# A hybrid decoder layer on one core: sums of y for the output projection from one load of each pair, and DRAM copies in rows of 8 KB

## The chip, the core and the metric

The kernel runs on one core of a Trainium2 chip. The core has five engines, each with its own queue of instructions that it works off in order: TensorE (PE; its weight loads are PEld) multiplies matrices into PSUM, VectorE (DVE) and ScalarE (ACT) do elementwise work, GpSimd (POOL) does some too and starts the DMAs that add into memory, and SyncE (SP) starts most of the other DMAs. Sixteen DMA engines move the data between DRAM and the on-chip memory (SBUF). The metric is the device time of one execution in microseconds, lower is better.

## The reference

One layer on 512 tokens with a model width of 2048, float32 throughout. Cut to what matters here:

```
h     = rms_norm(x, norm_w) * (1 + scale) + shift      # scale, shift, gate from c @ w_ada
proj  = h @ w_in                                       # split into aq ak av ag d_qkv dz db da mg_a mg_b
a_out = swa_attention(...) * silu(ag)
y_a   = a_out @ w_o_swa
o     = gated_delta_rule(...)                          # 32 value heads, chunks of 64 tokens
y_b   = (rms_norm(o) * silu(dz)) @ w_o_dn
y     = sigmoid(mg_a) * y_a + sigmoid(mg_b) * y_b      # 512 x 2048
out   = x + gate * (y @ w_out)                         # the output projection
```

## The kernel before

Each float32 factor of a large matmul is split in two, a high part (a rounding copy on ScalarE, line 52) and the rest (a subtraction on VectorE, line 53), and a product is three matmuls (`mm3`, lines 240 to 242): high by high, high by low, low by high. Weights come in tiles of 128 x 2048 (1 MB, `raw`, two buffers, line 200), are split in halves of 1024 columns (`whi`, `wlo`, three buffers), and every half feeds eight steps of 128 rows.

The stages in order: startup (adaLN, norm, first projections); DeltaNet (`deltanet`); the product with w_o_dn (`branch_b`); window attention (`attention`); `finish`. In the second part of DeltaNet the heads run in sixteen groups. While the matmuls of group g+1 stream, a chain of small scan steps of group g (`scan`: pp, pv, pd, po) is laid between them. `pump`, called after every six matmuls, advances such generators, and a generator with a rate advances only on a part of the calls.

One of these is `weight_sums`, started at group 2 with a rate of 0.13. It first copies x to the output in four DRAM-to-DRAM copies of 1 MB (line 671). Then it builds the summed weight quadrants of the output projection in DRAM (`ws_d`): for each of four parts two copies of a quadrant (line 684), two accumulating DMAs from GpSimd (line 688), one copy and one accumulation, and again one of each: 16 copies of 1 MB. They stand in SyncE's queue among the weight loads.

The output projection multiplies y (quadrants a11, a12 for the first 256 tokens, a21, a22 for the others, by halves of the 2048 columns) with w_out in seven products in place of eight, over two halves of the output columns n: m1 to m7 in the order of `out_order`, with a11, a12, the sums s3, s1, s2, then a22 and the sum s4. Each product is four items of twelve matmuls of 512 columns.

`finish` has two parts. The first, sixteen times, makes a tile of y: it loads the gate and the other branch's tile, takes the product with w_o_swa (`channel_tile`), combines them on VectorE (lines 1332, 1333), writes the tile to DRAM (`y_d`, line 1334), and splits its first 256 columns into a11 or a12; for the first eight tiles it also makes s3. s1, s2, s4 and a22 go to the memory of h (`hh`, `hl`), which is free only as the last of these products ends. So they are made in the second part, `output`, by `combos`, a generator that advances once per item: two passes over eight pairs of y tiles. GpSimd loads a pair from DRAM (line 1359, `ya` and `yc`, two buffers each), the first pass makes s1 and s2, the second loads the pair again and makes s4, and splits a22. An item's weights are split two items ahead by `prep`, and `out_load` (line 1395) loads w_out or its sums into three buffers. `evict` and `columns` combine the products, multiply with the gate and add into the output by DMA.

The order of the instructions on each engine isn't that of the code. A planner sets it when the program is built: it takes instructions in order of priority as they become ready by its own idea of how long things take, and allots the buffers. The blocks under `behind` (the scan steps, `weight_sums`) may not go ahead of the last matmul traced. On the chip each engine then keeps the order that was set, whatever is ready.

Of the kernel before, what the change touches and what calls it, by code (L numbers as in the profile page):

```python
# [36 lines left out]
class Layer:  # L37
# [628 lines left out]
    def weight_sums(self):  # L666

        nc = self.nc
        for t in range(NTB):
            s = slice(t * P, (t + 1) * P)  # L670
            nc.sync.dma_start(out=self.out[s], in_=self.a["x"][s])
            yield
        for n in range(2):
            for i in range(2):
                w = lambda c, r: self.a["w_out"][2 * c + n, 2 * r + i]
                m7, m5, m6, m4 = (self.ws_d[s, n, i] for s in ("m7", "m5", "m6", "m4"))
                steps = [
                    [(m7, w(1, 0), w(1, 1)), (m5, w(0, 0), w(1, 0))],
                    [(m6, m7, w(0, 0))],
                    [(m4, m6, w(0, 1))],  # L680
                ]
                for parts in steps:
                    for dst, src, _ in parts:
                        nc.sync.dma_start(out=dst, in_=src)
                    for _ in range(2):
                        yield
                    for dst, _, more in parts:
                        nc.gpsimd.dma_start(out=dst, in_=more, accum_op=ALU.add, max_dma_last_dim=8192)
                    for _ in range(2):
                        yield  # L690
# [621 lines left out]
    def finish(self):  # L1312
        tc, nc, a = self.tc, self.nc, self.a
        with ExitStack() as es:
            yp = es.enter_context(tc.tile_pool(name="fy", bufs=1, reuse_waits="tile"))
            wk = es.enter_context(tc.tile_pool(name="fwk", bufs=2, reuse_waits="tile"))
            quad = lambda pool, name: tuple(pool.tile([P, 8, 256], F32R, name=name + x) for x in "hl")
            A = {n: quad(yp, n) for n in ("a11", "s3", "a12")}
            self.wtiles, self.wnext = {}, 0
            self.wpool = es.enter_context(tc.tile_pool(name="fraw", bufs=3, reuse_waits="tile"))  # L1320
            for _ in range(3):
                self.out_load()
            lo, hi = slice(0, 256), slice(256, 512)
            with ExitStack() as eo:
                self.pmm = eo.enter_context(tc.tile_pool(name="pmmf", bufs=2, space=PSUM, reuse_waits="tile"))
                for j in range(KT):
                    m = wk.tile([P, T], F32, tag="m", name="m")
                    nc.sync.dma_start(out=m, in_=self.ma_d[j])
                    yb = wk.tile([P, T], F32, tag="yb", name="yb")
                    nc.sync.dma_start(out=yb, in_=self.yb_d[j])  # L1330
                    ps = self.channel_tile(f"os{j}")
                    nc.vector.scalar_tensor_tensor(out=m, in0=m, scalar=1.0, in1=ps, op0=ALU.add, op1=ALU.mult)
                    nc.vector.tensor_tensor(out=m, in0=m, in1=yb, op=ALU.add)
                    nc.sync.dma_start(out=self.y_d[j], in_=m)
                    h, l = A["a11" if j < 8 else "a12"]
                    self.split(h[:, j % 8, :], l[:, j % 8, :], m[:, lo])
                    if j < 8:
                        h, l = A["s3"]
                        nc.vector.tensor_tensor(out=yb[:, lo], in0=m[:, lo], in1=m[:, hi], op=ALU.add)
                        self.split(h[:, j, :], l[:, j, :], yb[:, lo])  # L1340
            v = lambda i: (self.hh[:, 4 * i : 4 * i + 4, :], self.hl[:, 4 * i : 4 * i + 4, :])
            for i, n in enumerate(("s1", "s2", "s4", "a22")):
                A[n] = tuple(x.rearrange("p a (b t) -> p (a b) t", b=2) for x in v(i))
            self.output(es, wk, A)

    def combos(self, wk, A):

        nc = self.nc
        lo, hi = slice(0, 256), slice(256, 512)
        TT = nc.vector.tensor_tensor  # L1350
        steps = [(second, kt) for second in range(2) for kt in range(8)]
        pairs = {}

        def load(i):
            if i < len(steps):
                kt = steps[i][1]
                for j, tag in enumerate(("ya", "yc")):
                    t = wk.tile([P, T], F32, tag=tag, name=tag)
                    nc.gpsimd.dma_start(out=t, in_=self.y_d[kt + 8 * j])
                    pairs[i, j] = t  # L1360

        load(0)
        load(1)
        yield
        for i, (second, kt) in enumerate(steps):
            p, q = pairs.pop((i, 0)), pairs.pop((i, 1))
            TT(out=p[:, hi], in0=p[:, hi], in1=q[:, hi], op=ALU.subtract)
            if second:
                TT(out=p[:, lo], in0=p[:, hi], in1=p[:, lo], op=ALU.add)
                TT(out=p[:, lo], in0=p[:, lo], in1=q[:, lo], op=ALU.subtract)  # L1370
                self.split(A["a22"][0][:, kt, :], A["a22"][1][:, kt, :], q[:, hi])
            else:
                nc.vector.scalar_tensor_tensor(
                    out=p[:, lo], in0=p[:, hi], scalar=-1.0, in1=p[:, lo], op0=ALU.mult, op1=ALU.subtract
                )
                self.split(A["s1"][0][:, kt, :], A["s1"][1][:, kt, :], p[:, hi])
            n = "s4" if second else "s2"
            self.split(A[n][0][:, kt, :], A[n][1][:, kt, :], p[:, lo])
            load(i + 2)
            yield  # L1380

    def out_order(self):
        return [
# [4 lines left out]
    def out_load(self):  # L1388
        j = self.wnext
        if j < 28:  # L1390
            n, m, i = j // 14, j // 2 % 7, j % 2
            name, _, q = self.out_order()[m]
            t = self.wpool.tile([P, 2048], F32, tag="raw", name="raww")
            src = self.a["w_out"][2 * q[0] + n, 2 * q[1] + i] if q else self.ws_d[name, n, i]
            self.nc.sync.dma_start(out=t, in_=src)
            self.wtiles[j] = t
            self.wnext += 1

    def output(self, es, wk, A):
# [7 lines left out]
        def prep(i):  # L1407
# [6 lines left out]
            if i % 2:  # L1414
                del self.wtiles[i // 2]
                self.out_load()

        side = self.combos(wk, A)
        next(side, None)
        todo = []  # L1420
# [15 lines left out]
        def evict(n, name):  # L1436
            TT = nc.vector.tensor_tensor
            for t in range(2):
                b = ps[name, t]
                if (n, name) == (1, "m4"):  # L1440
                    last[t] = wk.tile([P, T], F32, tag="yb", name="x")
                    nc.sync.dma_start(out=last[t], in_=a["x"][t * P : (t + 1) * P, 1024 + T : 2048])
                if name == "m1":
                    o = t * 1024 + n * T
                    nc.sync.dma_start(out=gt[:, t, :], in_=self.gate_d[o : o + T].partition_broadcast(P))
                if name in ("m1", "m5"):
                    k = wk.tile([P, T], F32, tag=f"{name}{t}", name=name, bufs=1)
                    nc.scalar.copy(out=k, in_=b)
                    keep[name, t] = k
                elif name == "m2":  # L1450
                    c = wk.tile([P, T], F32, tag="m", name="c11")
                    TT(out=c, in0=b, in1=keep["m1", t], op=ALU.add)
                    columns(n, 0, t, c, 1.0)
                elif name == "m6":
                    u1, u5 = keep["m1", t], keep["m5", t]
                    u = wk.tile([P, T], F32, tag="m", name="u2")
                    TT(out=u, in0=b, in1=u1, op=ALU.add)
                    TT(out=u1, in0=ps["m7", t], in1=u, op=ALU.add)
                    c = wk.tile([P, T], F32, tag="m", name="c22")
                    TT(out=c, in0=u1, in1=u5, op=ALU.add)  # L1460
                    TT(out=u5, in0=u, in1=u5, op=ALU.add)
                    columns(n, 1, 2 + t, c, 1.0)
                elif name == "m4":
                    k = keep["m1", t]
                    TT(out=k, in0=b, in1=k, op=ALU.subtract)
                    columns(n, 0, 2 + t, k, 1.0)
                elif name == "m3":
                    k = keep["m5", t]
                    TT(out=k, in0=b, in1=k, op=ALU.add)
                    columns(n, 1, t, k, -1.0, last.get(t) if n else None)  # L1470
# [133 lines left out]
```

## Time and profile before

| | us |
|---|---|
| median of 3 runs | 2958.47 (2956.22 to 2960.14) |
| the profiled execution | 2958.95 |
| its span, first to last instruction | 2956.1 |
| TensorE busy | 2884.4 |
| VectorE busy | 1750.1 |
| ScalarE busy | 1084.5 |
| GpSimd busy | 250.7 |

The mean granted clock of TensorE is 0.99 of full speed. A row of a timeline gives the start in us from the span's start, the duration, the engine, the line of the kernel, the operation with the tile it writes and those it reads, the shape, how many such instructions were merged, and in brackets how long the engine had been idle and what ended the idle time. A row of a group gives the number of instructions, then busy us and mean ns of one, then the idle time before them; or, in the view of a tile, the shortest, median and longest duration in ns. SPq stands for SyncE's queue of DMAs. A row of a stretch gives the busy time and, in parentheses, the number of instructions of each engine.

### The profile page before, as it was taken

What the parts mean: (1) busy time and instruction counts of PE and PEld (TensorE: products, weight loads), DVE (VectorE), ACT (ScalarE), POOL (GpSimd) and SP (SyncE); (2) the same over time, 40 slices, a digit from 0 to 9 for tenths busy, and PEclk for the clock granted to TensorE, in tenths of its full rate; (3) what the DMA queues carried; (4) which work ended last, traced back from release to release, by engine and by line L of the source; (5) the groups of instructions that cost most, each with busy time, mean ns of one, the idle gap of its engine ahead of it and who ended that gap; (6) DMA issues with size and microseconds to landing.
All of it is one profiled execution on the core that took longest, in us unless ns stands there. A gap on an engine that the chain in (4) does not pass through costs nothing.

```text
span 2956.1 us, 38061 instructions
## 1 busy us (share of the span) xinstructions
PE 2884.4 (98%) x14556; PEld 2359.3 (80%) x14556; DVE 1750.1 (59%) x2885; ACT 1084.5 (37%) x2113; POOL 250.7 (8%) x250
## 2 busy tenths in 40 slices
PE   8899999999899999999999999999999999999999
PEld 6677888887688888888888788888788788888777
DVE  7775998776677554545544453433755655554575
ACT  4354334332234433333333322311334434432343
POOL 0022211100101111110000000000100000000110
PEclk9999999999899999999999999999999999999999
DMA  9747555635456655754332575545322223365585
GB/s 384 278 147 222 168 155 168 190 110 183 146 156 181 201 181 158 205 157 140 113 123 87 200 265 195 200 165 165 105 83 99 76 88 111 109 249 181 175 250 170
DMA packets 175656, 497.78 MB, mean 168 GB/s; under 512 B 72978, under 2 KB 75538, under 8 KB 135602
## 3 DMA queue, kind: packets, MB, share of 16 engines
q1 hardware_dynamic: 168594, 466.52, 46.8%
q0 software_dynamic: 6880, 28.84, 4.7%
q8 instruction: 114, 1.87, 0.3%
q14 instruction: 68, 0.55, 0.1%
HBM read 433.61 MB, written 97.20 MB: 180 GB/s over the span
## 4 chain that ended last, share of the span: by engine, by line
PE 86%; DMA 2%; DVE 2%; issue 1%; ACT 1%; POOL 0%; SPq 0%; DVEq 0%; POOLq 0%; ACTq 0%
PE mm L240 24%; PE mm L242 24%; PE mm L241 24%; PE m L241 1%; PE m L242 1%; PE m L240 1%; PE S L1249 1%; PE pv L959 1%; PE po L978 1%; PE O L1300 1%; PE pP L274 1%; PE pd L974 1%; PE po L977 1%; PE pp L949 1%; DMA ya<-y_d 1%
## 5 line engine op out<-in xcount | busy, mean ns | idle before, releaser
L240 PE MATMUL mm<-hh,whi 128*128 128x512 f32 x2784 | 1133.4, 407 | 4.4 <-ACT whi L52 3.6
L242 PE MATMUL mm<-hh,wlo 128*128 128x512 f32 x2784 | 1093.1, 393 | 5.4 <-DVE wlo L53 5.4
L241 PE MATMUL mm<-hl,whi 128*128 128x512 f32 x2784 | 1090.5, 392 | 0.0
L53 DVE TENSOR_TENSOR wlo<-raw,whi 128x1024 fp32r<-128x1024 f32 (+1 forms) x428 | 526.7, 1234 | 506.4 <-ACT whi L52 490.2
L52 ACT CAST whi<-raw 128x1024 fp32r<-128x1024 f32 (+1 forms) x428 | 445.0, 1043 | 939.0 <-PE mm L241 908.5
L242 PEld LDWEIGHTS mm<-hh,wlo 128*128 128x128 f32 x2784 | 524.5, 188 | 122.0 <-DVE wlo L53 8.5
L240 PEld LDWEIGHTS mm<-hh,whi 128*128 128x128 f32 x2784 | 525.9, 189 | 115.6 <-issue 8.4
L241 PEld LDWEIGHTS mm<-hl,whi 128*128 128x128 f32 x2784 | 526.5, 189 | 99.6 <-issue 0.4
L240 PE MATMUL mm<-oh,whi 128*128 128x512 f32 x512 | 200.4, 393 | 2.0 <-ACT oh L52 1.0
L242 PE MATMUL mm<-oh,wlo 128*128 128x512 f32 x512 | 199.4, 390 | 0.5 <-DVE wlo L53 0.5
L241 PE MATMUL mm<-ol,whi 128*128 128x512 f32 x512 | 199.5, 390 | 0.3 <-DVE ol L53 0.3
L755 POOL TENSOR_TENSOR E<-E,neg_g 128x512 f32<-128x512 f32 x64 | 79.0, 1235 | 535.0 <-DMA E<-g_rows 386.7
L240 PEld LDWEIGHTS mm<-oh,whi 128*128 128x128 f32 x512 | 96.1, 188 | 23.8 <-ACT oh L52 1.9
L241 PEld LDWEIGHTS mm<-ol,whi 128*128 128x128 f32 x512 | 96.1, 188 | 22.2 <-DVE ol L53 1.4
L805 DVE TENSOR_TENSOR A<-A,atmp 128x62 f32<-128x62 f32 (+30 forms) x124 | 112.2, 905 | 1.7
L242 PEld LDWEIGHTS mm<-oh,wlo 128*128 128x128 f32 x512 | 96.1, 188 | 20.9 <-DVE wlo L53 1.2
L798 DVE TENSOR_TENSOR atmp<-A 128x62 f32<-128x62 f32 (+30 forms) x124 | 111.2, 896 | 1.5
L906 POOL TENSOR_TENSOR qe<-qe,yq 128x512 f32<-128x512 f32 x32 | 49.4, 1558 | 712.0 <-DMA qe<-eg_rows 495.7
L53 DVE TENSOR_TENSOR wlo<-raww,whi 128x1024 fp32r<-128x1024 f32 x56 | 68.5, 1222 | 33.1 <-ACT whi L52 33.0
L52 ACT CAST whi<-raww 128x1024 fp32r<-128x1024 f32 x56 | 58.8, 1052 | 62.1 <-PE m L242 54.4
L952 DVE SCALAR_TENSOR_TENSOR r<-pp,neg_eg,vt 128x128 f32<-128x128 f32 x96 | 29.3, 347 | 78.3 <-PE pp L949 77.1
L580 DVE SCALAR_TENSOR_TENSOR yv<-mm,convh,yv 128x511 f32<-128x511 f32 (+2 forms) x96 | 71.5, 745 | 4.2 <-ACT yv L576 2.6
(329 smaller groups left out, 3163.4 us busy)
## 6 DMA issues: line engine op xcount, KB each, us to landing
raw<-in_w_ch SPq DMA_DIRECT2D x158, 1024.0 KB
wa<-in_w_ada_ss SPq DMA_DIRECT2D x32, 1024.0 KB
raw<-in_w_od SPq DMA_DIRECT2D x32, 1024.0 KB
E<-g_rows SPq DMA_DIRECT2D x64, 256.0 KB
wsm<-in_w_out POOLq DMA_DIRECT2D x16, 1024.0 KB, 9.2
gw<-in_w_ada_gate SPq DMA_DIRECT2D x16, 1024.0 KB
raw<-in_w_os SPq DMA_DIRECT2D x16, 1024.0 KB
raww<-wsm SPq DMA_DIRECT2D x16, 1024.0 KB
```

What stands on the lines that cost most here:

```text
L52: self.nc.scalar.copy(out=hi, in_=src)
L53: self.nc.vector.tensor_tensor(out=lo, in0=src, in1=hi.bitcast(F32), op=ALU.subtract)
L240: nc.tensor.matmul(ps, lhsT=wh, rhs=xh, start=first, stop=False)
L241: nc.tensor.matmul(ps, lhsT=wh, rhs=xl, start=False, stop=False)
L242: self.last_mm = nc.tensor.matmul(ps, lhsT=wl, rhs=xh, start=False, stop=last).ins
L274: self.nc.tensor.transpose(dst[:, c * P : (c + 1) * P], src_cols(c), self.ident)
L580: nc.vector.scalar_tensor_tensor(out=y[:, s:], in0=ps[:, : T - s], scalar=w[:, j : j + 1], in1=y[:, s:], op0=ALU.mult, op1=ALU.add)
L755: nc.gpsimd.tensor_tensor(out=E, in0=E, in1=ng, op=ALU.add)
L798: eng.tensor_tensor(out=t, in0=A[:, m : m + 1, m + 1 :].to_broadcast([P, m, n]), in1=A[:, :m, m : m + 1].to_broadcast([P, m, n]), op=ALU.mult,
L805: eng.tensor_tensor(out=A[:, :m, m + 1 :], in0=A[:, :m, m + 1 :], in1=t, op=ALU.add)
L906: nc.gpsimd.tensor_tensor(out=qf, in0=qf, in1=q, op=ALU.mult)
L949: nc.tensor.matmul(pp, lhsT=kT[:, sl(c)], rhs=S, start=True, stop=True)
```

## The change

Three edits.

1. `combos` makes one pass. Each pair is loaded once, and s1, s2 and s4 are computed from it: s1 = a21 - a22, s2 = -s1 - a11, s4 = -s2 - a12. s2 and s1 lie beside each other, so that one split of 512 columns serves both; s4 has its own. The next pair but one is asked for after the split of s4, and there are eight steps in place of sixteen.
2. The quadrants that need no sum, a12 and a22, are both split in the first part of `finish`, in one split of 512 columns of the second eight tiles of y, into new tiles `right`. To make room, m1 and m5 are kept in the buffers `yb` and `ya`, and the pool of w_out tiles has two buffers and not three; the two `raw` buffers of the stages before serve as two more, by turns, so that two tiles are loaded ahead of the first part and two more at the start of `output`. The last two x tiles use the buffer `yc`.
3. The copies of `weight_sums` from SyncE, DRAM to DRAM, get `max_dma_last_dim=8192`: rows of 8 KB. The accumulating DMAs have it already.

```diff
@@ weight_sums
-            nc.sync.dma_start(out=self.out[s], in_=self.a["x"][s])
+            nc.sync.dma_start(out=self.out[s], in_=self.a["x"][s], max_dma_last_dim=8192)
...
-                        nc.sync.dma_start(out=dst, in_=src)
+                        nc.sync.dma_start(out=dst, in_=src, max_dma_last_dim=8192)
@@ finish
-            A = {n: quad(yp, n) for n in ("a11", "s3", "a12")}
+            A = {n: quad(yp, n) for n in ("a11", "s3")}
+            right = tuple(yp.tile([P, 8, T], F32R, name="right" + x) for x in "hl")
...
-            self.wpool = es.enter_context(tc.tile_pool(name="fraw", bufs=3, reuse_waits="tile"))
-            for _ in range(3):
+            self.wpool = es.enter_context(tc.tile_pool(name="fraw", bufs=2, reuse_waits="tile"))
+            for _ in range(2):
                 self.out_load()
...
-                    h, l = A["a11" if j < 8 else "a12"]
-                    self.split(h[:, j % 8, :], l[:, j % 8, :], m[:, lo])
-                    if j < 8:
+                    if j >= 8:
+                        self.split(right[0][:, j - 8, :], right[1][:, j - 8, :], m)
+                    else:
+                        h, l = A["a11"]
+                        self.split(h[:, j, :], l[:, j, :], m[:, lo])
                         h, l = A["s3"]
...
-            v = lambda i: (self.hh[:, 4 * i : 4 * i + 4, :], self.hl[:, 4 * i : 4 * i + 4, :])
-            for i, n in enumerate(("s1", "s2", "s4", "a22")):
-                A[n] = tuple(x.rearrange("p a (b t) -> p (a b) t", b=2) for x in v(i))
+            v = [x.rearrange("p (q a) (b t) -> p q (a b) t", q=4, b=2) for x in (self.hh, self.hl)]
+            for i, n in enumerate(("s2", "s1", "s4")):
+                A[n] = tuple(x[:, i] for x in v)
+            A["s21"] = tuple(x[:, 0:2] for x in v)
+            A["a12"], A["a22"] = (tuple(x[:, :, t] for x in right) for t in (lo, hi))
@@ combos
-        for i, (second, kt) in enumerate(steps):
-            p, q = pairs.pop((i, 0)), pairs.pop((i, 1))
+        for kt in range(8):
+            p, q = pairs.pop((kt, 0)), pairs.pop((kt, 1))
+            STT = nc.vector.scalar_tensor_tensor
             TT(out=p[:, hi], in0=p[:, hi], in1=q[:, hi], op=ALU.subtract)
-            if second:
-                TT(out=p[:, lo], in0=p[:, hi], in1=p[:, lo], op=ALU.add)
-                TT(out=p[:, lo], in0=p[:, lo], in1=q[:, lo], op=ALU.subtract)
-                self.split(A["a22"][0][:, kt, :], A["a22"][1][:, kt, :], q[:, hi])
-            else:
-                nc.vector.scalar_tensor_tensor(
-                    out=p[:, lo], in0=p[:, hi], scalar=-1.0, in1=p[:, lo], op0=ALU.mult, op1=ALU.subtract
-                )
-                self.split(A["s1"][0][:, kt, :], A["s1"][1][:, kt, :], p[:, hi])
-            n = "s4" if second else "s2"
-            self.split(A[n][0][:, kt, :], A[n][1][:, kt, :], p[:, lo])
-            load(i + 2)
+            STT(out=p[:, lo], in0=p[:, hi], scalar=-1.0, in1=p[:, lo], op0=ALU.mult, op1=ALU.subtract)
+            STT(out=q[:, lo], in0=p[:, lo], scalar=-1.0, in1=q[:, lo], op0=ALU.mult, op1=ALU.subtract)
+            h, l = (x[:, :, kt, :] for x in A["s21"])
+            self.split(h, l, p.rearrange("p (b t) -> p b t", b=2))
             yield
+            self.split(A["s4"][0][:, kt, :], A["s4"][1][:, kt, :], q[:, lo])
+            if kt < 6:
+                load(kt + 2)
@@ out_load
-            t = self.wpool.tile([P, 2048], F32, tag="raw", name="raww")
+            t = (self.wraw if j // 2 % 2 else self.wpool).tile([P, 2048], F32, tag="raw", name="raww")
@@ output
+        for _ in range(2):
+            self.out_load()
         side = self.combos(wk, A)
...
-                    last[t] = wk.tile([P, T], F32, tag="yb", name="x")
+                    last[t] = wk.tile([P, T], F32, tag="yc", name="x")
...
-                    k = wk.tile([P, T], F32, tag=f"{name}{t}", name=name, bufs=1)
+                    k = wk.tile([P, T], F32, tag="yb" if name == "m1" else "ya", name=name)
```

More of the change, by code (lines that the diff above doesn't have):

```diff
@@ L1350, in combos, with load @@
         TT = nc.vector.tensor_tensor
-        steps = [(second, kt) for second in range(2) for kt in range(8)]
         pairs = {}
[L1354 to L1360, printed above, removed]
+        def load(kt):
+            for j, tag in enumerate(("ya", "yc")):
+                t = wk.tile([P, T], F32, tag=tag, name=tag)
+                nc.gpsimd.dma_start(out=t, in_=self.y_d[kt + 8 * j])
+                pairs[kt, j] = t
         load(0)
```

## The prediction

> **What bounds the kernel now.** I read the page first, then busy time by stretches, then the chain of waits in the two places where TensorE is not full, and there the order of each engine. A line of the page and seven stretches (columns: start and end, length, busy us of PE, PEld, DVE, ACT, POOL with counts, granted clock, DMA share, GB/s):
>
> ```profile
> PE 2884.4 (98%) x14556; PEld 2359.3 (80%) x14556; DVE 1750.1 (59%) x2885; ACT 1084.5 (37%) x2113; POOL 250.7 (8%) x250
> ...
> 700.00:740.00 40.00, 33.49 (x157) 25.78 (x155) 17.39 (x31) 9.25 (x27) 1.84 (x2) 0.87 0.47 131
> 740.00:780.00 40.00, 29.30 (x95) 22.20 (x96) 21.77 (x33) 9.45 (x21) 3.39 (x4) 0.70 0.21 73
> 820.00:860.00 40.00, 40.00 (x202) 33.63 (x201) 27.66 (x52) 16.09 (x40) 6.03 (x6) 1.00 0.43 139
> 2606.00:2782.00 176.00, 175.23 (x774) 144.76 (x773) 78.90 (x114) 48.75 (x70) 5.48 (x10) 1.00 0.58 195
> 2782.90:2821.70 38.80, 35.07 (x145) 27.84 (x144) 28.62 (x52) 18.69 (x30) 9.40 (x17) 0.96 0.80 257
> 2821.70:2850.00 28.30, 23.38 (x90) 18.23 (x90) 17.85 (x31) 12.14 (x19) 3.78 (x7) 0.88 0.66 232
> 2850.00:2949.70 99.70, 99.70 (x440) 82.23 (x439) 64.76 (x72) 38.19 (x39) 10.44 (x12) 1.00 0.70 202
> ```
>
> TensorE is the bound at 98%, and most stretches are full. Two are not, and both touch the diff: 700 to 780 us, in the DeltaNet heads just after the first DRAM copies, and 2783 to 2850, in the output projection. A gain can only be idle time or slow clock taken back there.
>
> **The first place.** The chain of waits gives the start of the same step (pqk) in successive head groups:
>
> ```profile
> 627.30 0.89 PE pqk L910 x8
> 694.62 0.89 PE pqk L910 x8
> 794.54 0.89 PE pqk L910 x8
> 861.85 0.89 PE pqk L910 x8
> ```
>
> The periods are 67.3, 99.9 and 67.3 us: one group costs 32.6 us more than its neighbours. The SyncE queue and ScalarE there (columns of these and the later timeline rows: start, duration, engine, line, operation; in brackets the idle time before and what ended it), and DMA traffic in the stretch between:
>
> ```profile
> 663.96 1.26 SPq L671 DMA_DIRECT2D out<-in_x  x2
> 677.19 0.33 SPq L200 DMA_DIRECT2D raw<-in_w_ch  x1
> ...
> 689.79 1.70 SPq L671 DMA_DIRECT2D out<-in_x  x1
> 691.59 0.53 SPq L200 DMA_DIRECT2D raw<-in_w_ch  x1
> 692.16 0.52 SPq L671 DMA_DIRECT2D out<-in_x  x1
> 718.13 0.33 SPq L200 DMA_DIRECT2D raw<-in_w_ch  x1
> 718.50 1.13 SPq L684 DMA_DIRECT2D wsm<-in_w_out  x2
> ...
> 700.00:715.00 15.00, 12.53 (x72) 9.61 (x71) 6.32 (x13) 3.83 (x10) 0.00 (x0) 0.97 0.00 0
> ...
> 713.41 1.99 ACT L52 CAST whi<-raw 128x1024 fp32r<-128x1024 f32 x2
> 740.83 1.98 ACT L52 CAST whi<-raw 128x1024 fp32r<-128x1024 f32 x2
> ```
>
> The weights asked for at 677.19 and 691.59 have landed by 700: for 15 us nothing moves. Yet ScalarE splits them at 713.41 and 740.83, behind scan steps, both halves in a row, so TensorE has scan steps with no weight matmuls between. No transfer is waited for; the order of the instructions, fixed at build time by the planner, puts the splits late, as it would if it took the loads for late. What this group has and the ones before it have not is the four copies of x to the output in the same queue, two ahead of the load at 677.19 and one right ahead of that at 691.59.
>
> **The second place.** The output projection's matmuls:
>
> ```profile
> 2782.87 0.39 PE L240 MATMUL m<-whi,a11h 128*128 128x512 f32 x1
> ...
> 2799.43 0.50 PE L241 MATMUL m<-wlo,a12h 128*128 128x512 f32 x1 [2.56 <-DVE wlo L53]
> 2800.15 0.63 PE L240 MATMUL m<-whi,a12h 128*128 128x512 f32 x1
> 2800.57 0.63 PE L241 MATMUL m<-wlo,a12h 128*128 128x512 f32 x1
> ...
> 2821.75 0.39 PE L240 MATMUL m<-whi,hh 128*128 128x512 f32 x1
> 2829.62 0.50 PE L240 MATMUL m<-whi,hh 128*128 128x512 f32 x1 [2.27 <-ACT whi L52]
> 2832.35 0.80 PE L241 MATMUL m<-wlo,hh 128*128 128x512 f32 x1 [2.22 <-DVE wlo L53]
> ...
> 2949.34 0.39 PE L242 MATMUL m<-whi,hl 128*128 128x512 f32 x1
> ```
>
> Undisturbed, 440 of them take 99.7 us (last stretch above): 0.2266 apart. 14 products of 48 matmuls need 152.3 us; first to last start took 166.5, so 14.2 are lost. By 2821.75, 144 matmuls in (32.6 us), 6.2 are lost; the other 8.0 fall in the second pass of sums. What is late in front of the splits:
>
> ```profile
> 2797.02 0.43 DVE L1367 TENSOR_TENSOR ya<-ya,yc 128x256 f32<-128x256 f32 x1 [4.56 <-DMA ya<-y_d]
> 2828.22 0.40 ACT L52 CAST hh<-yc 128x256 fp32r<-128x256 f32 x1 [5.53 <-DMA yc<-y_d]
> ```
>
> VectorE and ScalarE stand at a sum whose y pair has not landed, and the weight split queued behind comes late.
>
> **The change part by part. Sums in one pass.** An item is 12 matmuls, 2.72 us. VectorE per item now: its weight split and the sums.
>
> ```profile
> L53 DVE TENSOR_TENSOR wlo<-raww,whi 128x1024 fp32r<-128x1024 f32 x56 | 68.5, 1222 | 33.1 <-ACT whi L52 33.0
> ...
> L53 DVE TENSOR_TENSOR hl<-ya,hh x24: 415/420/425, 2775.0 to 2845.4; 128x256 fp32r<-128x256 f32 x24
> L1367 DVE TENSOR_TENSOR ya<-ya,yc x16: 417/424/426, 2714.4 to 2841.7; 128x256 f32<-128x256 f32 x16
> ...
> L1333 DVE TENSOR_TENSOR m<-m,yb x16: 691/693/693, 2623.9 to 2783.8; 128x512 f32<-128x512 f32 x16
> ```
>
> First pass: 1.22, two sums of 0.42 (the second has the shape of L1367's), two splits of 0.42: 2.90 us; second pass, with three sums, 3.32. Sixteen items: 49.8 us of VectorE against 43.5 of TensorE. After: eight steps of three sums, one 512-wide split (0.69, by the row of L1333) and one of 256: 1.22 + 1.27 + 0.69 + 0.42 = 3.60, then eight items of 1.22: 38.6 us. Half of the y loads go, 16 of 32 on POOL's queue; the load of pair kt+2 is asked for a step later than now, after the last split of pair kt. I price the second pass at its whole loss, 8.0 us, as nothing of it is left. The first pass keeps its 6.2: two pairs are loaded ahead as before, six still wait for a buffer. Bounds: all 14.2 go, or none: six steps exceed the item by 0.88, a backlog of 5.3 us, of which a split's slack (two items less its 2.3 us on two engines, 3.1) hides part; 2.2 stay, and a stall drags slow matmuls behind it, 0.43 apart by the starts at 2800.15 and 2800.57, as the clock is down; for the nine or so of the first stall that is 1.8 us. Twice such a 4 us takes the 8.0 back.
>
> [...]
>
> **Splits moved into the gating stage.** Eight tiles split 512 columns, not 256: 0.27 us of VectorE each (0.69 less 0.42), 2.2 us in all if laid bare. From 2606 to 2782 VectorE is busy for 78.9 us of 176, ScalarE for 48.75, TensorE for 175.23: nothing.
>
> **Weight buffers.** Two of w_out ahead of the stage, not three, and two more in the other pool after it. If the third load stands in SyncE's queue behind the last y write, it is late for the second product:
>
> ```profile
> 2774.05 0.38 SPq L1442 DMA_DIRECT2D x<-in_x  x1
> ...
> 2784.52 0.33 SPq L1334 DMA_DIRECT2D y_d<-m  x1
> ...
> wsm<-in_w_out POOLq DMA_DIRECT2D x16, 1024.0 KB, 9.2
> ```
>
> At 9.2 us for 1 MB it would land at 2794.0; it must be there by 2791.4 (2793.75, four items in, less 2.3 for the split, 1.0 on ScalarE and 1.22): 2.6 us at worst. The first row, a load that the code asks for in the second half of the projection, shows that the queue's order follows the buffers, and these come free with the last splits of the gating stage: nothing. From then on one load more is in flight; no gain, as no matmul waits for these loads. The x tiles, now in a buffer that the sums free near 2812 (eight steps of 3.60 from 2783), are needed at the very end; the kept m1 and m5 have the lifetimes that they had.
>
> **Copies in rows of 8 KB.** 24 copies of 1 MB. On the engines their price is small: the load at 718.13 and both copies behind it are through when the first accumulate starts:
>
> ```profile
> 726.14 1.03 POOL L688 DMA_DIRECT2D wsm<-in_w_out  x1 [38.80 <-DMA wsm<-in_w_out]
> ```
>
> That is 3 MB in at most 8 us, all beside TensorE: directly 0 either way. The order is what can move. Bounds: 0, or the whole 32.6, or a loss (below). The weight loads have 8 KB rows themselves, and nowhere else does the order hold them for late; a copy cut like them is nearest to them. I take the 32.6.
>
> Sum: 2958.95 (the profiled execution, 0.5 over the median of 2958.47) - 32.6 - 8.0 = 2918.3, against the median 2918.
>
> **The rivals.** *The order stays.* The later copies of w_out have the old rows too, and the stretches beside them, such as 820 to 860, are full. That speaks against copies as the cause; the x copies alone are suspect, and rows may not be what the planner minds. Then 2958.5 - 8.0 = 2950, 2944 to 2956.
> [...]
> *Slower: the order comes to hold more loads for late.* A copy has more rows, and if the planner charges by row, the loads behind the wsm pairs go the way of this one. Three loads were split late in the gap: 10.9 us each. With the gap kept and the gain of 8.0, the first further late load decides; the three later pairs would give 2950 + 33 = 2983. For it: orders are unstable, and this one is off once already. Against it: the pairs are harmless now.
> *Gap gone, but the heavier steps eat the output gain:* 2926.
>
> **How the numbers follow.** Forecast 0.55, order stays 0.23, slower 0.17, output gain eaten 0.05. The forecast's own range is 2911 (14.2 regained) to 2926 (none). The range: 2910 to 2956, which leaves out the slower case. Measurement tells 0.2%, 5.9 us: the stays case passes that in about seven of ten. Faster 0.55 + 0.05 + 0.16 = 0.76, same 0.07, slower 0.17.
>
> **What would show it.** The pqk steps 67.3 us apart throughout, and ScalarE's splits one by one between 694 and 770: the copies were it. A period near 100 anywhere: they were not, or moved. In the output stage no wait on ya or yc after about 2815 on the old scale, and first-to-last matmul near 158 us; over 166 says that one pass costs more than two. Idle TensorE at the second product <- raw tiles would mean the third load. Wrong altogether if new idle time stands in a stretch that is full now.

## The result, and the profile after

| | before | after |
|---|---|---|
| median, us | 2957.34 (2953.45 to 2960.14, 4 runs) | 2920.91 (2917.23 to 2922.19, 4 runs) |
| the profiled execution | 2958.95 | 2922.19 |
| its span | 2956.1 | 2919.7 |
| first to last start of the output projection's matmuls | 166.5 | 159.3 |
| last pqk step | 1602.32 | 1571.97 |

The ratio is 0.9876, 95% interval 0.9859 to 0.9893: 36.4 us are saved. The forecast was 2918, 2.9 us below.

The first place. The chain of waits of the changed kernel gives pqk at:

```profile
628.10 0.89 PE pqk L910 x8
763.98 0.89 PE pqk L910 x8
```

The step between these two rows is not on the chain, so 135.88 us stand for two groups, and two periods of 67.3 make 134.6. Before, the same two groups took 167.24 (627.30 to 794.54): 31.4 us came back. SyncE's queue, ScalarE's splits and the stretches of 40 us there:

```profile
678.12 0.55 SPq L200 DMA_DIRECT2D raw<-in_w_ch  x1
680.15 0.58 SPq L671 DMA_DIRECT2D out<-in_x  x1
...
706.33 0.34 SPq L200 DMA_DIRECT2D raw<-in_w_ch  x1
706.72 0.56 SPq L671 DMA_DIRECT2D out<-in_x  x1
...
709.47 1.05 ACT L52 CAST whi<-raw 128x1024 fp32r<-128x1024 f32 x1 [0.57 <-PE mm L241]
715.39 1.05 ACT L52 CAST whi<-raw 128x1024 fp32r<-128x1024 f32 x1 [2.14 <-PE mm L241]
...
700.00:740.00 40.00, 39.85 (x206) 33.16 (x205) 30.43 (x45) 14.11 (x31) 1.85 (x2) 1.00 0.70 209
740.00:780.00 40.00, 39.21 (x217) 32.06 (x217) 30.40 (x50) 15.19 (x31) 7.86 (x7) 1.00 0.55 178
```

The copies of x now lie one by one between weight loads, and the splits come one by one some 6 to 7 us apart, where they came in twos at 713 and 741. TensorE is busy for 39.85 of 40 us (33.49 before) and its granted clock, 0.87 and 0.70 before, is 1.00.

The second place. TensorE's first and last rows of the output projection, its stalls between, two of VectorE's waits, and the stage in two stretches:

```profile
2753.72 0.39 PE L240 MATMUL m<-whi,a11h 128*128 128x512 f32 x1
...
2770.67 0.50 PE L241 MATMUL m<-wlo,righth 128*128 128x512 f32 x1 [2.33 <-DVE wlo L53]
2771.01 0.40 PE L242 MATMUL m<-whi,rightl 128*128 128x512 f32 x1
2771.24 0.40 PE L240 MATMUL m<-whi,righth 128*128 128x512 f32 x1
...
2784.28 0.50 PE L241 MATMUL m<-wlo,s3h 128*128 128x512 f32 x1 [2.32 <-DVE wlo L53]
...
2790.89 0.50 PE L241 MATMUL m<-wlo,s3h 128*128 128x512 f32 x1 [0.81 <-DVE wlo L53]
...
2913.00 0.39 PE L242 MATMUL m<-whi,hl 128*128 128x512 f32 x1
...
2768.60 0.43 DVE L1370 TENSOR_TENSOR ya<-ya,yc 128x256 f32<-128x256 f32 x1 [2.86 <-DMA yc<-y_d]
...
2782.67 0.42 DVE L1370 TENSOR_TENSOR ya<-ya,yc 128x256 f32<-128x256 f32 x1 [2.83 <-DMA yc<-y_d]
...
2753.70:2790.90 37.20, 31.71 (x135) 24.36 (x133) 27.99 (x48) 18.98 (x27) 6.04 (x10) 1.00 0.61 212
2790.90:2913.00 122.10, 122.10 (x539) 101.08 (x539) 75.18 (x81) 47.55 (x49) 10.36 (x12) 1.00 0.68 200
```

From 2790.89 on TensorE is never idle again (last stretch); what is left, some 7 of the 14.2 us, lies in the first 37 us, where the weight split (line 53) comes late because VectorE stood before it at a sum whose yc had not landed. (At the third stall, 2790.89, VectorE has worked without a gap since the second wait; it is still catching up.) The stage begins 29.15 us earlier (2782.87 before) and is 7.2 us shorter.

### The profile page after: what moved, and what is told of

Same layout as the page of the kernel before. It is cut to its first block, busy times and chain, and to the rows that moved or that the text cites. A ratio compares the mean times of both kernels' runs of the same rounds, so it can differ in the third digit from the quotient of the medians.

```text
span 2919.7 us, 37991 instructions
## 1 busy us (share of the span) xinstructions
PE 2868.2 (98%) x14556; PEld 2349.8 (80%) x14556; DVE 1740.0 (60%) x2853; ACT 1082.6 (37%) x2097; POOL 243.5 (8%) x234
## 3 DMA queue, kind: packets, MB, share of 16 engines
q8 instruction: 114, 1.87, 0.3%
## 4 chain that ended last, share of the span: by engine, by line
PE 87%; DVE 5%; issue 4%; ACT 2%; DMA 2%; POOL 1%; SPq 0%; DVEq 0%; POOLq 0%; ACTq 0%
PE mm L240 24%; PE mm L242 23%; PE mm L241 23%; PE m L241 1%; PE m L242 1%; PE m L240 1%; DVE wa L414 1%; PE S L1249 1%; PE pv L959 1%; PE po L978 1%; PE O L1300 1%; PE pP L274 1%; DVE wlo L53 1%; PE pd L974 1%; PE po L977 1%
## 5 line engine op out<-in xcount | busy, mean ns | idle before, releaser
L1273 ACT ACTIVATE sm<-sm,mx,rs 128x256 f32<-128x256 f32 (+1 forms) x128 | 71.7, 562 | 3.3 <-DVE mx L1268 3.3
```

The source lines that it names most:

```text
L1273: nc.scalar.activation(t, t, AF.Exp, scale=r[:, h : h + 1], bias=mx[:, h : h + 1], accum_out=den[:, h : h + 1])
```

## The experiments

In the tables of this section "loss" is first to last start of the output projection's matmuls less 152.1 us, the length that three of the kernels below show with no loss at all; counted so, the kernel before loses 14.4 and the changed one 7.2. (The prediction's 14.2, taken against 152.3, and the expectations' 6.9 and 5.4 come out 0.2 to 0.3 below this count.)

### Which edit gives what

e2_sums is the changed kernel without the two `max_dma_last_dim=8192` on SyncE's copies:

```diff
-  nc.sync.dma_start(out=self.out[s], in_=self.a["x"][s], max_dma_last_dim=8192)
+  nc.sync.dma_start(out=self.out[s], in_=self.a["x"][s])
-  nc.sync.dma_start(out=dst, in_=src, max_dma_last_dim=8192)
+  nc.sync.dma_start(out=dst, in_=src)
```

> The kernel before with the sums of the output projection in one pass, the wider splits and the weight buffers, and all 24 DRAM copies in their old rows. Theory (the copies' rows and the sums are two separate gains): the group with period 99.9 us stays and only the output stage shortens, by 7 to 8 us: about 2950. Rival (the gap goes with anything that changes the order of instructions a little, the rows are no cause): the periods are 67.3 us throughout and the time is about 2920, that of the changed kernel. If the gain of the output stage needs the rows: about 2957.

e3_xrows is the kernel before with the first of these lines alone in its new form, e4_wrows with the second alone:

```diff
 e3_xrows
-  nc.sync.dma_start(out=self.out[s], in_=self.a["x"][s])
+  nc.sync.dma_start(out=self.out[s], in_=self.a["x"][s], max_dma_last_dim=8192)
 e4_wrows
-  nc.sync.dma_start(out=dst, in_=src)
+  nc.sync.dma_start(out=dst, in_=src, max_dma_last_dim=8192)
```

> The kernel before with only the four copies of x to the output in rows of 8 KB. Theory (these four rows alone set the order that makes the gap): all steps pqk 67.3 us apart, ScalarE's weight splits one by one between 694 and 770 us, 31 us saved: about 2926. Rival (the rows of the copies of w_out count too): some of the gap stays, 2930 to 2957. The output stage keeps its 14.2 us of loss by both.

> The kernel before with only the 20 copies of w_out in DRAM in rows of 8 KB; TensorE, VectorE, ScalarE and GpSimd have the same instructions in the same order as before, so this measures the rows on the DMA engines alone. Theory (the transfers were never waited for, the rows act through the order only): no change, 2957 within 3 us. Rival (long rows hold up the loads of weights behind them, so short ones win): faster by some us, with the period of 99.9 us shortened; if short rows cost more, slower.

e5_xpool keeps the old rows and moves the copies of x to another queue:

```diff
-  nc.sync.dma_start(out=self.out[s], in_=self.a["x"][s])
+  nc.gpsimd.dma_start(out=self.out[s], in_=self.a["x"][s])
```

> The kernel before with the four copies of x in their old rows of 64 KB, but issued by GpSimd and not by SyncE. Theory (what matters is which loads the order takes for late behind the copies in SyncE's queue; the transfers themselves are harmless): the gap goes, periods of 67.3 us, about 2926. Rival (rows of 64 KB on the DMA engines delay the weights, from whatever queue): the gap stays and the time is about 2957.

| | us | ratio to before, 95% | period before the gap + at it | loss |
|---|---|---|---|---|
| e2_sums | 2949.44 | 0.9971 (0.9959 to 0.9982) | 67.31 + 99.25 | 8.2 |
| e3_xrows | 2926.06 | 0.9896 (0.9881 to 0.9910) | 67.31 + 68.29 | 13.9 |
| e4_wrows | 2957.17 | 1.0001 (0.9992 to 1.0011) | 67.29 + 99.79 | 14.4 |
| e5_xpool | 2927.41 | 0.9902 (0.9886 to 0.9919) | 67.30 + 67.31 | 13.1 |

The chain of waits of e2_sums (two rows), e3_xrows and e5_xpool, and for e5_xpool two of the copies in GpSimd's queue:

```profile
692.64 0.89 PE pqk L910 x8
791.89 0.89 PE pqk L910 x8
```

```profile
692.83 0.89 PE pqk L910 x8
761.12 0.89 PE pqk L910 x8
```

```profile
693.45 0.89 PE pqk L910 x8
760.76 0.89 PE pqk L910 x8
...
686.12 1.03 POOL L671 DMA_DIRECT2D out<-in_x  x2
```

The two gains are separate and add: the sums give 7.6 us with the gap in place, the rows of four copies give 31.0 us with the old output stage. The sum, 38.6, and the 36.4 of both together differ by less than the intervals allow. The rows of the copies of w_out (the trace has 16, not the 20 of the expectations) give nothing, and as e4_wrows has the order of instructions of the kernel before on TensorE, VectorE, ScalarE and GpSimd, this is the price of these rows on the DMA engines alone: 0.0001, and the interval reaches 0.0011. In e5_xpool all 20 copies have their old rows (its execution counts 175655 DMA packets, the kernel before 175656; the four of x are 64 packets of 64 KB there) and the gap is gone, so the long rows did no harm here, as such or by their traffic (0.9902). They acted through what the order does with the weight loads around them in SyncE's queue.

### Does the gap follow the copies?

e6_xlate issues the four copies of x, unchanged, after the copies of w_out:

```diff
 def weight_sums(self):
-    for t in range(NTB):
-        s = slice(t * P, (t + 1) * P)
-        nc.sync.dma_start(out=self.out[s], in_=self.a["x"][s])
-        yield
     for n in range(2):
         ...
+    for t in range(NTB):
+        s = slice(t * P, (t + 1) * P)
+        nc.sync.dma_start(out=self.out[s], in_=self.a["x"][s])
+        yield
```

> The kernel before with the four copies of x, in their old rows of 64 KB and in SyncE's queue, issued after the 20 copies of w_out and not ahead of them. Theory (the long rows make the order hold the weight loads around them for late, wherever they stand): the group with a period near 100 us moves from the third to about the twelfth, all periods before it are 67.3 us, and the time stays near that of the kernel before, 2945 to 2957. Rival (the gap belongs to its place, where the first copies join the heads): the gap goes and the time is about 2926, or it stays where it was.

Measured: 2965.62 us, 1.0024 of the kernel before (1.0015 to 1.0034). Its chain of waits, SyncE's queue and ScalarE's splits:

```profile
1301.73 0.89 PE pqk L910 x8
1388.30 1.72 PE pqk L910 x8
1470.93 0.89 PE pqk L910 x8
...
1301.54 0.34 SPq L200 DMA_DIRECT2D raw<-in_w_ch  x1
1301.94 0.52 SPq L689 DMA_DIRECT2D out<-in_x  x1
1311.08 0.34 SPq L200 DMA_DIRECT2D raw<-in_w_ch  x1
...
1340.33 1.98 ACT L52 CAST whi<-raw 128x1024 fp32r<-128x1024 f32 x2
1365.79 1.98 ACT L52 CAST whi<-raw 128x1024 fp32r<-128x1024 f32 x2
1388.82 2.94 ACT L52 CAST whi<-raw 128x1024 fp32r<-128x1024 f32 x3
```

The gap has moved with the copies to groups 12 and 13, 86.57 and 82.63 us, 34.6 above two periods of 67.3. Around 700 us there is none left. The picture is that of the kernel before: loads asked for beside the copies, at 1301.54 and 1311.08, are split 30 us and more later, in clusters of two, two and three. The time missed my upper bound of 2957 by 8.6 us: the gap is 2 us wider than in the kernel before, and at the start of the output projection (2789.40 against 2782.87) the kernel is 6.5 us behind. Some 3 us of that came after the last group and are not explained.

### How large is one late cluster?

e7_x2of4 gives the new rows to the first two copies of x only:

```diff
-  nc.sync.dma_start(out=self.out[s], in_=self.a["x"][s])
+  nc.sync.dma_start(out=self.out[s], in_=self.a["x"][s], **({} if t >= 2 else dict(max_dma_last_dim=8192)))
```

> The kernel before with the first two copies of x in rows of 8 KB and the last two in the old rows of 64 KB. Instead of two stretches of 8 and 19 scan steps without a weight matmul, the order has one of 14 (5 is the usual number). Theory (the time lost goes with the scan steps that stand alone): (14 - 5) of (8 - 5) + (19 - 5) = 17, about half of 31 us, so 2941. Rival (each row of 64 KB costs on the DMA engines): as e4 and e5 showed no cost of long rows, 2926; if any two of them are harmless, 2926 too; if the whole gap stays, 2957.

Measured: 2934.80 us, 0.9925 (0.9910 to 0.9940). Its chain of waits and its late cluster of ScalarE's splits, and behind these the third cluster of the kernel before:

```profile
627.86 0.89 PE pqk L910 x8
772.07 0.89 PE pqk L910 x8
...
743.51 2.93 ACT L52 CAST whi<-raw 128x1024 fp32r<-128x1024 f32 x3
...
766.43 2.93 ACT L52 CAST whi<-raw 128x1024 fp32r<-128x1024 f32 x3
```

Two groups take 144.21, 9.6 above two periods, and not half of the gap. My theory, 2941, failed: the count of lone scan steps doesn't give the time. What fits these three kernels is the number of clusters in which splits come late: one here (743.51) for 9.6 us, three before (713, 741, 766) for 32.6, three in e6_xlate for 34.6: 9.6 to 11.5 us each, near the 10.9 that the prediction took for a late load in its slower rival. On TensorE each cluster ends a stretch without a weight matmul, from the last one's start to the next one's: 10.6 us here, 6.4, 12.7 and 8.7 before, 13.3, 8.7 and 7.8 in e6_xlate. e3_xrows, e5_xpool and the changed kernel have none above 4.5 us between 560 and 900.

### What is left in the output stage

e8_noload is the changed kernel in which six pairs aren't loaded again:

```diff
             if kt < 6:
-                load(kt + 2)
+                for j in range(2):
+                    pairs[kt + 2, j] = (p, q)[j]
```

> The changed kernel with the loads of the y pairs 2 to 7 left out: the sums of these steps take the tiles of pairs 0 and 1 again, as they were left, so the sums and splits are all still made but of other numbers, and the output is not the reference's. It parts the two causes of the 6.9 us that the output stage still loses. Theory (VectorE stands waiting for yc, whose buffer comes free only after the last split of its pair): 2 us or less are lost, about 2916. Rival (VectorE has too much to do, 3.60 us a step for 2.72 us of TensorE): the loss stays near 5 to 7 us, 2919 to 2921.

e9_yc3 loads everything, but sooner:

```diff
-        def load(kt):
-            for j, tag in enumerate(("ya", "yc")):
-                t = wk.tile([P, T], F32, tag=tag, name=tag)
+        def load(kt, js=(0, 1)):
+            for j in js:
+                tag = ("ya", "yc")[j]
+                t = wk.tile([P, T], F32, tag=tag, name=tag, bufs=2 + j)
         load(1)
+        load(2, (1,))
             self.split(h, l, p.rearrange("p (b t) -> p b t", b=2))
+            if kt < 6:
+                load(kt + 2, (0,))
             yield
             self.split(A["s4"][0][:, kt, :], A["s4"][1][:, kt, :], q[:, lo])
-            if kt < 6:
-                load(kt + 2)
+            if kt < 5:
+                load(kt + 3, (1,))
```

> The changed kernel with a third buffer for yc, so that its load is asked for a step earlier, and the load of ya asked for right behind the split that frees its buffer, half a step earlier. Nothing is left out. Theory (the waits for yc make the weight splits late): the stalls at 2771 and 2784 us shrink or go, 3 to 6 us saved, 2915 to 2918. Rival (VectorE's load): 2921, as the changed kernel. If ya becomes the late one instead: 2919 to 2921 with the waits on ya.

e10_gt adds a buffer, the one of the gate tile, in which pair 2 is loaded at the start; e11_act and e13_sync are e9_yc3 with the pairs' loads on another queue; TensorE has the same order in all three, VectorE and ScalarE have not:

```diff
 e10_gt
+                if kt == 2:
+                    if j == 0:
+                        gts[1] = wk.tile([P, 2, T], F32, tag="gt", name="yg", bufs=1)
+                    t = gts[1][:, j, :]
 e11_act
-                nc.gpsimd.dma_start(out=t, in_=self.y_d[kt + 8 * j])
+                nc.scalar.dma_start(out=t, in_=self.y_d[kt + 8 * j])
 e13_sync
-                nc.gpsimd.dma_start(out=t, in_=self.y_d[kt + 8 * j])
+                nc.sync.dma_start(out=t, in_=self.y_d[kt + 8 * j])
```

> The kernel of e9_yc3 with one more pair loaded ahead: pair 2 lies in the buffer of the gate tile, which is needed only from the fifth item on. Nothing is left out. Without the loads (e8_noload) nothing at all is lost in the output stage, and e9_yc3 still lost 5.4 us, half of it behind a late ya of the last pair. Theory (it is the round from buffer free to pair landed, some 5 us by the median from issue to landing, that a third pair hides): a loss of 0 to 3 us, 2914 to 2917. Rival (the last pairs still stand behind the two buffers of ya, whatever is loaded first): as e9_yc3, 2918.

> The kernel of e9_yc3 with the loads of the pairs issued by ScalarE and not by GpSimd. Theory (the landing takes some 5 us of the round, and much of that is the way through GpSimd's queue): a shorter landing, a loss of 1 to 4 us, 2914 to 2917. Rival (a load queued on ScalarE waits there for the split of VectorE that frees its buffer, and the casts of the weights wait behind it): 2920 to 2930. If the queue makes no difference: 2918.

> The changed kernel itself, for a comparison with e10_gt on the same chip: 2921, 0.9876 of the kernel before.

> The kernel of e9_yc3 with the loads of the pairs issued by SyncE; TensorE has the order of e9_yc3 and e11_act. It asks why ScalarE's queue took the loss away. Theory (the way through GpSimd's queue costs the round a few us, any other queue is as good as ScalarE's): 2913 to 2916, a loss under 2 us. Rival (SyncE's queue also carries the loads of w_out, which stand there for up to 22 us until a buffer is free, and the y loads behind them come late): 2918 to 2930.

| | us | ratio to before, 95% | loss |
|---|---|---|---|
| e12_after, the changed kernel again | 2921.80 (2921.11 to 2922.50) | 0.9877 (0.9862 to 0.9892) | 7.3 |
| e8_noload | 2913.44 (2912.56 to 2916.06) | 0.9855 (0.9838 to 0.9871) | 0.0 |
| e9_yc3 | 2918.15 (2917.02 to 2920.59) | 0.9869 (0.9855 to 0.9884) | 5.6 |
| e10_gt | 2917.01 (2914.05 to 2919.16) | 0.9858 (0.9841 to 0.9874) | 3.9 |
| e11_act | 2913.45 (2912.72 to 2914.64) | 0.9849 (0.9834 to 0.9864) | 0.0 |
| e13_sync | 2912.21 (2910.67 to 2916.01) | 0.9851 (0.9834 to 0.9867) | 0.0 |

e8_noload decides between the two causes: with all sums and splits in place and no loads, nothing is lost, so VectorE has not too much to do. The 7.2 us come from waits for pairs. e9_yc3 moved these rather than ended them (2918.15, at the edge of the 2915 to 2918 of its theory), and e10_gt, with one more pair loaded ahead, still loses 3.9 where 0 to 3 were expected. The longest stall of e9_yc3, the wait behind it, and the two loads before it in GpSimd's and SyncE's queues:

```profile
2776.24 0.50 PE L241 MATMUL m<-wlo,righth 128*128 128x512 f32 x1 [2.88 <-DVE wlo L53]
...
2774.16 0.42 DVE L1372 TENSOR_TENSOR ya<-ya,yc 128x256 f32<-128x256 f32 x1 [2.98 <-DMA ya<-y_d]
...
2768.08 0.54 POOL L1362 DMA_DIRECT2D ya<-y_d  x1 [1.80 <-DVE hl L53]
...
2760.68 6.85 SPq L1397 DMA_DIRECT2D raww<-wsm  x2
```

The last ya is asked for at 2768.08 and its sum starts at 2774.16, 6.1 us later; the second of the two 1 MB weight loads had left SyncE's queue half a microsecond earlier. In e11_act and e13_sync nothing stalls. The output stage of e11_act as one stretch, its longest wait for a pair, and in ScalarE's queue the ya of that wait and the last ya:

```profile
2752.70:2904.86 152.16, 152.16 (x673) 125.92 (x671) 101.79 (x124) 65.91 (x73) 12.22 (x14) 1.00 0.70 211
...
2764.79 0.42 DVE L1372 TENSOR_TENSOR ya<-ya,yc 128x256 f32<-128x256 f32 x1 [2.15 <-DMA ya<-y_d]
...
2759.80 0.33 ACTq L1362 DMA_DIRECT2D ya<-y_d  x1
2770.38 0.33 ACTq L1362 DMA_DIRECT2D ya<-y_d  x1
```

And SyncE's queue of e13_sync:

```profile
2767.40 0.32 SPq L1362 DMA_DIRECT2D ya<-y_d  x1
...
2769.20 0.32 SPq L1397 DMA_DIRECT2D raww<-wsm  x1
```

Neither rival came about. Nothing on TensorE waits in e11_act, and in e13_sync the last ya stands 1.8 us ahead of the next weight load; one yc does stand right behind a weight load (2762.82 behind 2762.44), but nothing waits for it. Both kernels beat the changed one: on the same chip e11_act's slowest run, 2914.64, is below e12_after's fastest, 2921.11, and e13_sync's slowest on another chip, 2916.01, is below 2917.23, the fastest run of the changed kernel anywhere.

Why the queue matters is only half settled. Issuing a load took 0.33 us on ScalarE's queue and 0.32 on SyncE's in place of GpSimd's 0.54, at 0.33 that is 3.4 us for 16 loads, and most of these lay beside other work. What the traces show is that a small load landed later close behind a large one. In the output stage of the changed kernel, the six loads of a pair's tile issued at most 1.4 us behind a weight load of 1 MB landed after 4.3 to 5.9 us, the six others after 2.9 to 3.6. Another queue didn't spare a load this: the ya of e11_act issued at 2759.80, 0.6 us behind a weight load, was used 5.0 us later, and one of e13_sync, as close behind one (2758.57), 5.7 us later. But the last ya, 0.9 us behind a weight load in e9_yc3, is 4.0 and 5.0 us behind one in these two, and is used 3.5 and 4.4 us after its issue in place of 6.1. VectorE's order changed as well, and it still waits 2.15 and 1.87 us for a ya there while TensorE waits for nothing. So queue, place and order changed together, and how much each of them brings stays open.

## Why the prediction was right, point by point

**The gap and its cause.** Right, and now shown, not only argued: the rows of the four x copies, not those of w_out (e3, e4); by way of the order around SyncE's queue, not by the transfers (e5); in another place too (e6). The rival *order stays* fell with the gap, and the gain isn't one of the transfers: with an equal order the rows of the w_out copies make 0.0001 (e4). How the planner arrives at a different order for long rows was not tried; that two of four copies still make one cluster (e7) is all the runs say.

**Its size.** Priced 32.6, measured 31.4: the two groups that the gap spans take 1.3 us above two periods. Every kernel without the gap has such a rest in these groups: e3_xrows has one period of 68.29, e5_xpool one of 68.13 a group later. What it is was not looked for.

**The sums in one pass.** Priced at 8.0, measured 7.2 (in e2_sums 6.2 of the stage and 7.6 of the time). Right in place as well: no loss after 2790.89, which is 2820 on the old scale (29.15 later), as the second pass's loss is gone. But the agreement is in part luck, as the prediction cut the old loss in the wrong place. It gave all that was lost by 2821.75, 6.2 us, to the first pass. VectorE and TensorE of the kernel before show the second pass at work before that (line 1369 belongs to it alone):

```profile
2805.42 0.43 DVE L1367 TENSOR_TENSOR ya<-ya,yc 128x256 f32<-128x256 f32 x1 [2.56 <-DMA ya<-y_d]
2805.88 0.42 DVE L1369 TENSOR_TENSOR ya<-ya 128x256 f32<-128x256 f32 x1
...
2807.50 0.50 PE L241 MATMUL m<-wlo,a12h 128*128 128x512 f32 x1 [0.76 <-DVE wlo L53]
```

The split that TensorE waits for at 2807.50 stands behind these sums. Until then 4.5 us were lost, so of the 14.4 us the first pass cost 4.5 and the second 9.9. The one pass of the changed kernel costs 7.2, not what the old first pass did but 2.7 more, in two long stalls without slow clock in place of one with it. The gain is 9.9 less 2.7, and it comes out near 8.0 because the prediction took the first 1.9 too low and put the second at nothing.

What failed is a reason given beside it. The upper bound of cost rested on VectorE's 3.60 us a step against 2.72 of an item, "a backlog of 5.3 us". e8, e11 and e13 do the same VectorE work and lose nothing; two of the eight steps' splits are through before the stage begins (VectorE's rows at 2747.10 and 2750.53, two splits each), and the waits for the pairs, with the work that piles up behind them, are the whole of the loss.

**A stall's price.** The prediction's upper bound of cost put 1.8 us of slow clock behind a stall of 2.2 us, twice, taken from the matmuls 0.43 us apart behind the 2.56 us of idle time that ends at 2799.43. That did not come: the stalls of 2.33 and 2.32 us in the changed kernel have no slow clock behind them (matmuls 0.23 us apart at 2771.01 and 2771.24, a clock of 1.00 over the stretch). In e2_sums a stall of 3.06 us, at 2813.05, has: the matmuls from 2814.82 to 2817.38 are 0.43 apart. The last section comes back to this.

**Wider splits, third weight load, x tiles, kept m1 and m5, copies on the DMA engines.** All priced at nothing. From the last pqk to the start of the output projection the changed kernel takes 1181.75 us and the one before 1180.55; e4_wrows, with the order of the kernel before, takes 1181.65. So 1 us there is the scatter of executions. The stretch of the gating stage is full:

```profile
2570.00:2745.00 175.00, 174.25 (x769) 143.99 (x768) 82.40 (x113) 52.83 (x70) 2.26 (x4) 1.00 0.59 205
```

The stalls of the output projection that are left end with a split held up by a pair, or by VectorE catching up behind one, none with a late tile of w_out. Two readings there were wrong without a consequence: the copies are 20 and not 24 (4 of x, 16 for w_out), and the 3 MB beside 718.13 took 9.6 us and not 8, as the second copy's packets ran until 727.76, past the start of the accumulate.

**The sum.** 40.6 us were forecast, 36.4 came. Between the profiled executions the heads, from the first pqk to the last, give 30.9 us and the output stage 7.2; 0.5 goes before the first pqk (559.70 against 559.16) and 1.2 between the last pqk and the output projection. That makes 36.4, the difference of the spans. The 1.7 us before and between the two places are of the size by which the same stages differ from kernel to kernel (the first pqk of these kernels starts at 557.2 to 559.7). *Slower: more loads late* and *output gain eaten* did not come about, though e6_xlate shows that a late cluster elsewhere was a real danger, at the price given.

## What to carry to other kernels

A stage that is slow with neither a transfer nor an engine to blame may have its order wrong: look for splits or loads that come in clusters, ask which instruction beside them the neighbouring groups don't have, and test it by changing that instruction's shape, its queue and its place in turn. Test hardware and order apart: a variant that changes the transfers and keeps the order of the instructions (here the rows of w_out) says what the transfer itself costs. When a load waits for a buffer, a further buffer may only move the wait (e9_yc3 and e10_gt still lost 5.6 and 3.9 us); try the queue and see which large load the small one stands behind (here 4.3 to 5.9 us to landing close behind one, 2.9 to 3.6 otherwise).

## What the runs showed of the hardware that was not expected

The length of a TensorE stall alone did not set whether the clock fell. Before, 2.56 us of idle time was followed by matmuls 0.43 us apart (rows at 2800.15 and 2800.57; a clock of 0.60 from 2800 to 2804), and in e2_sums 3.06 us was; in e9_yc3 a stall between the two, the 2.88 us ahead of the row at 2776.24, was not:

```profile
2776.58 0.40 PE L242 MATMUL m<-whi,rightl 128*128 128x512 f32 x1
2776.82 0.40 PE L240 MATMUL m<-whi,righth 128*128 128x512 f32 x1
...
2772.00:2776.00 4.00, 1.35 (x6) 0.75 (x4) 1.80 (x3) 0.92 (x2) 0.00 (x0) 1.00 0.27 106
2776.00:2780.00 4.00, 3.76 (x16) 3.11 (x17) 4.00 (x8) 2.86 (x4) 0.00 (x0) 1.00 0.63 229
```

The granted clock stayed at 1.00 through 2.88 us of idle time. And it also fell with no long stall at all. In the gap of the kernel before, TensorE was busy for 4.12 of the 6.6 us from 708 on and never idle for more than 0.98 us at a time, and yet the next stretch has half the clock:

```profile
714.60:721.00 6.40, 5.42 (x13) 3.76 (x12) 5.74 (x7) 1.88 (x3) 0.00 (x0) 0.50 0.22 77
```

What decides it beside the length, no run shows.

Rows of 64 KB and of 8 KB moved in DRAM-to-DRAM copies at no difference that the time could tell: 16 copies of 1 MB beside other work, 1.0001 (0.9992 to 1.0011).
